# Input stage of a gated attention block: rows turned by diagonal matmuls, a second copy of x already transposed, and two more gate chunks computed there

## The chip, the cores and the metric

One NeuronCore of a Trainium2 chip runs the whole kernel. The metric is the device time of one execution in microseconds, lower is better; it is given as the median of repeated runs.

## The reference

The block takes x of 2048 tokens by 1024 features. All matrices and x are float32. In short:

```python
h = rms_norm(x, norm_gain)                      # per token, then a gain per feature
proj = h @ w_in                                 # 1024 -> 8448 columns
qa, ka, va, qb, kb, vb, ga, gb, mg = split(proj)
ya = banded_attention(qa, ka, va, ...) * silu(ga)      # ga: 512 columns
yb = three_dilated_groups(qb, kb, vb, ...) * silu(gb)  # gb: 512 columns
gates = sigmoid(mg + b_merge)                   # two gates of 1024 columns
merged = gates[0] * (ya @ w_branch_a) + gates[1] * (yb @ w_branch_b)
out = x + merged @ w_out
```

The columns of ga and gb, 1024 in all, are cut into eight **gate chunks** of 128. The change moves chunks 2 and 3 (the second half of ga).

## The kernel before, in words

Every large product is made in float16 with both factors split into a high and a low half: XH and XL hold the normed x, transposed (feature chunks of 128 on the partitions, 2048 tokens along the free axis), and a product takes three matmuls: high by high, high by low, low by high. The program has four stages, one after the other on PE.

**Input stage.** It makes XH and XL and computes gate chunks 0 and 1. x arrives in 16 slabs of 128 tokens (`x_load`), with two gate weights (`g_load`) and the first unit's weights among them. For a slab: ACT squares it with a sum (`x_square`), DVE and ACT make the reciprocal root (`x_stats`, `x_guess`, `x_newton`), DVE multiplies the slab by that and by the gain in one pass of 1024 columns (`x_scale`), PE transposes it in eight blocks through the identity matrix (`x_turn`), ACT copies each half of four blocks to XH (`x_hi`), DVE subtracts to get XL (`x_lo`). Between these PE works on eight gate steps (`g_step`): a chunk of 128 columns over a quarter of 512 tokens, 24 matmuls of 512 columns each. After a step ACT takes the tanh, DVE forms (1 + tanh) times the projection (`gate_steps`), and SP stores the result to DRAM (gtd). The order of all this is set by a small planner, `class Order`: each step has an engine, a cost, the steps it waits for and a rank; the planner lays them out in time and emits the instructions in that order. Each engine then works strictly in the order emitted.

**Main stage.** Units of heads: projection, attention, and, per 128 columns of the attention's output, a turned copy to DRAM (ytd). `YPart` multiplies chunks 0 and 1 by their stored gates there; chunks 2 to 7 go to ytd without their gate.

**Tail.** The table SEQ lists groups (dc, q): dc 0 to 7 are the merge gates, dc 8, 9 and 10 the gate chunks 2 to 7, two chunks of 128 columns to a dc. A group covers 256 columns by 1024 tokens by seven half-size products of 12 matmuls, 84 matmuls of 512 columns. After the products of a group with dc of 8 or more, `silu` loads the matching block of ytd, applies the gate on ACT and DVE, notes its maximum, and stores it. A second planner, `class Plan`, sets the order. K_AT says over which groups the 16 pieces of branch and output weights are prepared.

**Branch stage.** It multiplies by the branch and output weights and ends the program. Its scale y0 needs the maxima of all gated chunks.

Of the kernel before, what the change touches and what calls it, by code (L numbers as in the profile page):

```python
# [21 lines left out]
F32 = mybir.dt.float32  # L22
# [17 lines left out]
VSC = 2.0 ** -16  # L40
SX = 2.0 ** 8
# [43 lines left out]
STD, W_EARLY, G_TH, G_SI, G_CP, K_AT = 5.2, 24.0, 2.0, 4.0, 1.0, (4, 17)  # L85
# [5 lines left out]
X_LD = ("g", 0, 1, 2, 3, "w0", 4, 5, "w1", 6, 7, 8, 9, 10, 11, 12, 13, "u")  # L91
X_RK = (-35, 21, 20, -9)
X_TR = 0.6
X_NR = (-34, -92, 28)
X_XR = (7, -126, 40, 10)
X_GR = (29, 49)
X_TWO = (0, 1, 2, 2)
X_GF = (6.6, 15.2)
X_TH = (45, 46, 85, 86, 125, 126, 165, 166)
X_US = dict(look=0.25, land=4.3, next=1.45, late=.12, sq=1.14, st=.17, ln=.2, nw=.75, sc=1.24, tr=.8, hi=.5, lo=.62, gs=2.1, pw=1.3,  # L100
            gh=1.06, gl=1.26, mm=.217, th=.6, gt=.63, us=.83, uh=.75, ul=.82, ag=1.0, tl=1.3)
X_AG, H_AT = .9, (.1, .35)
XT_BUFS = 14
# [7 lines left out]
def block_kernel(tc, x, w_units, w_gate, w_mrg, w_out, w_bra, w_brk, gain, qkg, sink, bias_a, bias_b, b_merge, out):  # L111
# [166 lines left out]
    gtd = [dr.tile([128, S], F32, name=f"gtd{c}") for c in range(2)]  # L278
# [46 lines left out]

    def g_sum(c):
        gw[c][3] = norm_sum(gw[c][3][:], 1)

    def g_pow(c):
        raw, gh, gl, ps = gw[c]  # L330
        s, inv = norm_pow(ps)
        ih = ucol()
        V.tensor_scalar(ih[:], inv[:], 0.5 / SX, gp2[0][:], OP.mult, OP.mult)
        gw[c] = (gh, gl, ih, raw, s)

    def g_hi(c):
        gh, gl, ih, raw, s = gw[c]
        A.activation(gh[:], raw, AF.Copy, scale=s[:])

    def g_lo(c):  # L340
        gh, gl, ih, raw, s = gw[c]
        V.scalar_tensor_tensor(gl[:], raw, s[:], gh[:], OP.mult, OP.subtract)
        done.add(("g", c))

    def g_step(c, q):

        gh, gl, ih = gw[c][:3]
        ps = pj_p.tile([128, 512], F32, name="pj")
        ts = slice(512 * q, 512 * q + 512)
        out = []  # L350
        for w, xx in ((gh, XH), (gh, XL), (gl, XH)):
            for ch in range(NCH):
                i = len(out)
                out.append(lambda w=w, xx=xx, ch=ch, i=i: T.matmul(  # L354
                    ps[:], lhsT=w[:, ch, :], rhs=xx[:, ch, ts], start=(i == 0), stop=(i == 23)))
        return out, gate_steps(ps, c, q, ih, None)

    def gate_steps(ps, c, q, ih, m):
        th = []

        def tanh():
            th.append(gp.tile([128, 512], F32, name="yo", bufs=3))
            if m is None:
                A.activation(th[0][:], ps[:], AF.Tanh, scale=ih[:])
# [47 lines left out]
    sp0 = st.enter_context(tc.tile_pool(name="sp0", bufs=1))  # L412
    qg = cst.tile([128, 4, HD], F32, name="qg")
# [20 lines left out]

    groups = {t: tuple(i for i in range(4) if X_TWO[i] == X_TWO[t]) for t in range(4)}
    groups.update((t, tuple(range(t - t % 4, t - t % 4 + 4))) for t in range(4, NT))

    def x_square(t):
        g = groups[t]
        if t == g[0]:  # L440
            xss[g] = [sm.tile([128, 4], F32, name="xss")]
        jk = sp0.tile([128, D], F16, name="jk")
        A.activation(jk[:], xts[t][:], AF.Square, accum_out=xss[g][0][:, t - g[0]:t - g[0] + 1])

    def x_stats(g):
        ss = xss[g][0][:, :len(g)]
        V.tensor_scalar(ss, ss, 1.0 / (D * SX * SX), EPS / (SX * SX), OP.mult, OP.add)
        xss[g] = [ss]

    def x_guess(g):  # L450
        if g[0] == 12:
            A.preload_act_table_set("natural_log_exp_and_others")
        xss[g].append(rs_guess(xss[g][0], len(g)))

    def x_newton(g):
        ss, y = xss[g]
        xss[g] = sm.tile([128, 4], F32, name="xr")
        r = xss[g][:, :len(g)]
        rs_newton(ss, y, r, len(g), False)
        V.tensor_scalar(r, r, gi2[0][:], None, OP.mult)  # L460
# [5 lines left out]
    gb = sp0.tile([128, D], F32, name="gb")  # L466

    def gain_load():
        nc.sync.dma_start(out=gb[:], in_=gain.broadcast_to([128, D]))

    def gain_scale():
        m = sm.tile([128, 1], F32, name="gm")
        V.tensor_reduce(m[:], gb[:], AX.X, OP.max, apply_absolute_value=True)
        s, i = pow2(m[:], "x")
        gp2.append(ucol())
        gi2.append(ucol())
        V.tensor_scalar(gp2[0][:], i[:], 2.0 ** 14, None, OP.mult)
# [38 lines left out]
    class Order:  # L516


        def __init__(self):
            self.steps, self.end, self.free, self.on = {}, {}, {}, {}  # L520

        def add(self, name, eng, us, deps, rank, f, *args, first=0.0):
            assert name not in self.steps
            self.on[name] = eng
            self.steps[name] = (eng, us, deps, rank, f, args, first)

        def start(self, name):
            eng, _, deps, _, _, _, first = self.steps[name]
            if any(d not in self.end for d in deps):
                return None  # L530
            late = X_TR if name[0] == "tr" and name[1] > 3 else X_US["late"]
            return max([first, self.free.get(eng, 0.0)] + [self.end[d] + (0 if self.on.get(d) == eng else late) for d in deps])

        def run(self):
            while self.steps:
                best = {}
                for n, s in self.steps.items():
                    t = self.start(n)
                    if t is not None:
                        best.setdefault(s[0], []).append((t, s[3], n))  # L540
                eng, c = min(best.items(), key=lambda e: min(e[1])[0])
                t0 = min(c)[0]
                t, _, n = min((x for x in c if x[0] <= t0 + (0 if eng == "T" else X_US["look"])), key=lambda x: x[1])
                eng, us, _, _, f, args, _ = self.steps.pop(n)
                self.end[n] = self.free[eng] = t + us
                at(t, f, *args)

    od = Order()
    us_ = X_US
    n = 0  # L550
    for k in X_LD:
        for i in range(4 if k == "u" else 1):
            f, args = {"g": (gain_load, ()), "u": (w_load, (0, (i,)))}.get(k, (x_load, (k,)))
            if k in ("w0", "w1"):
                f, args = g_load, (int(k[1]),)
            at(.001 * n, f, *args)
            od.end["ld", k, i] = us_["land"] + us_["next"] * n
# [1596 lines left out]
```

## Time and profile before

| | |
|---|---|
| median of three runs | 1904.86 us (1904.34 to 1906.05) |
| span of the profiled execution, first to last instruction | 1902.2 us |
| time of the profiled execution itself | not listed apart; the median lies 2.7 us above its span |
| PE busy | 1871.2 us, 98% of the span |
| DVE, ACT, POOL busy | 79%, 66%, 31% |
| chain that ended last, by engine | PE 91%, DMA 5%, DVE, ACT and issue 1% each |
| first matmul of the main stage | 80.74 us |

A busy share is the time in which an engine had an instruction in flight. The chain is followed back from the last instruction: at each step to what released it. A timeline row gives its start and duration in us, then engine, line, operation, output and inputs, shape, count, and in brackets the idle time before it and what ended that.

### The profile page before, as it was taken

How to read it: one execution, taken by the hardware profiler on the slowest of the kernel's cores; microseconds unless marked ns; L12 is line 12 of the kernel's file. 1: busy time of each engine (PE TensorE's matmuls, PEld its weight loads, DVE VectorE, ACT ScalarE, POOL GpSimd, SP SyncE). 2: the span in 40 equal slices, each digit the busy share in tenths (PEclk: the TensorE clock that was granted, in tenths of full speed). 3: DMA queues.
4: the chain of work that ended last, by engine and by line, in shares of the span. 5: the costliest groups of instructions: out<-in, count | busy, mean ns of one | idle time of the engine just before them, and what ended most of it. 6: DMA issues, size and time to landing. Idle time of an engine off the chain costs nothing.

```text
span 1902.2 us, 51103 instructions
## 1 busy us (share of the span) xinstructions
PE 1871.2 (98%) x19254; PEld 1439.5 (76%) x19254; DVE 1499.1 (79%) x3837; ACT 1249.0 (66%) x3015; POOL 581.6 (31%) x1363
## 2 busy tenths in 40 slices
PE   6999999999999999999999999999999999999999
PEld 4568987889999899998999899544444446776775
DVE  7679878986886889878789888748779644987885
ACT  8478768886777777777777766565666865433341
POOL 0034343443453435543455444300000000322121
PEclk9999999999999999999999999999999999999999
DMA  6259998987888779888897777776666648854442
GB/s 257 83 103 203 168 194 137 199 168 157 171 148 180 140 155 202 146 166 176 142 176 145 146 153 134 172 300 184 202 201 187 191 154 274 295 162 121 143 149 76
DMA packets 638983, 326.21 MB, mean 171 GB/s; under 512 B 458768, under 2 KB 589712, under 8 KB 636304
## 3 DMA queue, kind: packets, MB, share of 16 engines
q1 hardware_dynamic: 638592, 322.69, 73.1%
q8 instruction: 150, 2.46, 0.6%
q14 instruction: 97, 0.79, 0.1%
q10 hardware_dynamic: 144, 0.26, 0.0%
HBM read 139.08 MB, written 73.66 MB: 112 GB/s over the span
## 4 chain that ended last, share of the span: by engine, by line
PE 91%; DMA 5%; DVE 1%; ACT 1%; issue 1%; SPq 0%; POOL 0%; DVEq 0%; POOLq 0%
PE pj L693 43%; PE fps L1607 18%; PE fps L1927 8%; PE fps L2012 7%; PE s L846 5%; PE pv L895 4%; PE pj L354 2%; DMA pt<-p 2%; PE pj L306 2%; DMA kq<-spl 1%; PE fps L306 1%; PE pt L959 1%; DMA bigl<-sd 1%; DMA graw<-in_w_gate_dram 0%; PE s L484 0%
## 5 line engine op out<-in xcount | busy, mean ns | idle before, releaser
L693 PE MATMUL pj<-wl,XH 128*128 128x128 f16 (+2 forms) x2816 | 715.2, 268 | 0.0
L693 PE MATMUL pj<-wh,XL 128*128 128x128 f16 (+2 forms) x2816 | 711.6, 269 | 0.0
L693 PE MATMUL pj<-wh,XH 128*128 128x128 f16 (+2 forms) x2816 | 708.6, 268 | 0.0
L693 PEld LDWEIGHTS <-XH 128*128 128x128 f16 x5632 | 574.9, 112 | 54.1
L693 PEld LDWEIGHTS <-XL 128*128 128x128 f16 x2816 | 315.8, 112 | 23.8
L861 DVE CUSTOM_DVE_ANT_0 pr<-s,b,ubuf 128x256 f32<-128x256 f32 (+3 forms) x512 | 218.7, 464 | 39.1 <-PE s L846 36.1
L878 DVE SCALAR_TENSOR_TENSOR p<-pr,p 128x512 f16<-128x512 f32 (+2 forms) x256 | 195.9, 765 | 49.7 <-ACT p L874 48.4
L760 POOL TENSOR_TENSOR rw<-rw,g 128x128 f32<-128x128 f32 (+1 forms) x224 | 149.2, 686 | 198.8 <-DVE rw L753 177.8
L1937 POOL TENSOR_TENSOR g<-g,t 128x512 f32<-128x512 f32 x32 | 48.4, 1514 | 522.1 <-DVE t L1859 521.6
L1607 PEld LDWEIGHTS <-wh 128*128 128x128 f16 x1064 | 104.2, 99 | 123.4 <-issue 0.3
L711 ACT ACTIVATE rw<-pj 128x256 f32<-128x256 f32 (+1 forms) x224 | 87.4, 390 | 135.8 <-PE pj L693 135.3
L775 POOL COPY spl<-spl 128x256 f16<-128x256 f16 (+1 forms) x224 | 97.4, 464 | 241.8 <-DVE spl L770 241.8
L874 ACT ACTIVATE p<-pr 128x512 f16<-128x512 f32 (+2 forms) x256 | 157.6, 616 | 10.7 <-DMA pt<-p 6.3
L846 PE MATMUL s<-kq 128*128 128x128 f16 (+1 forms) x1984 | 151.1, 217 | 2.7 <-DMA kq<-spl 1.6
L1927 PE MATMUL fps<-y,bigh 128*128 128x128 f16 x1792 | 153.4, 219 | 0.0
L1927 PE MATMUL fps<-y,bigl 128*128 128x128 f16 x896 | 151.7, 219 | 0.0
L2012 PE MATMUL fps<-WO,mf 128*128 128x512 f16 x660 | 147.5, 379 | 0.0
L846 PEld LDWEIGHTS <-kq 128*128 128x128 f16 x2016 | 131.0, 98 | 18.9 <-issue 3.5
L1927 PEld LDWEIGHTS <-bigh 128*128 128x128 f16 x1792 | 139.0, 98 | 7.3
L895 PE MATMUL pv<-vt,pt 128*128 128x65 f16 (+1 forms) x2784 | 131.6, 193 | 5.7 <-DMA pt<-p 5.7
L895 PEld LDWEIGHTS <-pt 128*128 128x128 f16 x3024 | 119.5, 97 | 21.0 <-DMA pt<-p 8.1
L766 ACT ACTIVATE spl<-rw 128x512 f16<-128x512 f32 (+1 forms) x112 | 72.0, 643 | 79.3 <-POOL vt L722 67.4
(255 smaller groups left out, 3804.6 us busy)
## 6 DMA issues: line engine op xcount, KB each, us to landing
wraw<-in_w_units_dram SPq DMA_DIRECT2D x56, 384.0 KB, 4.5
g<-mgd SPq DMA_DIRECT2D x64, 256.0 KB, 5.1
wraw<-in_w_mrg_dram SPq DMA_DIRECT2D x45, 256.0 KB, 4.3
mgd<-t SPq DMA_DIRECT2D x43, 256.0 KB, 2.8
zd<-z SPq DMA_DIRECT2D x128, 66.0 KB, 2.0
zz<-zd SPq DMA_DIRECT2D x64, 132.0 KB, 3.4
xt<-in_x_dram SPq DMA_DIRECT2D x16, 512.0 KB, 8.0
ytd<-yo SPq DMA_DIRECT2D x32, 256.0 KB, 3.3
```

What stands on the lines that cost most here:

```text
L693: out.append(lambda lhs=lhs, rhs=rhs, ch=ch, a=a, b=b, k=k: T.matmul(ps[:, a:b], lhsT=lhs[:, ch, :], rhs=rhs[:, ch, a:b], start=(k == 0), ...
L711: A.activation(self.rw[:, n * i:n * i + n], self.ps[i][:, :n], AF.Copy)
L760: G.tensor_tensor(q[:, i, :un.nq, :], q[:, i, :un.nq, :], g, OP.mult)
L775: G.tensor_copy(sp[:, i, nh:, :, :], sp[:, i, nq:nh, ::-1, :])
L846: T.matmul(self.sv[j][:, o:o + k1 - k0], lhsT=q[:, h, :], rhs=kt[:, un.nq + kh + v * un.nk, k0:k1], start=(v == 0), stop=(v == 1))
L861: V.tensor_tensor_reduce(out=self.pv[:, j, self.p0:self.p0 + W], in0=self.sv[j], in1=un.bias[:, self.h0 + j, self.b0:self.b0 + W], scale=I ...
L874: A.activation(self.sp[:, :128 * n], self.pr, AF.Copy, scale=PSC)
L878: V.scalar_tensor_tensor(self.sp[:, 128 * n:], self.pr, PSC, self.sp[:, :128 * n], OP.mult, OP.subtract)
L895: T.matmul(self.po[:, j, :w], lhsT=p[:, n * j + s, :], rhs=un.v[key][:, vh, c0:c0 + w], start=(k == 0 and s == 0), stop=(k == 2 and s == n ...
L1607: T.matmul(b[k][:], lhsT=w[:, i, ch, :], rhs=xform(PROD[i][0], lo, ch, q), start=(i < 3 and n == 0), stop=(n == 11), skip_group_check=True)
L1927: out.append(lambda p=p, c=c, wl=wl, yl=yl, n=n: T.matmul(ps[:, 128 * p:128 * p + 128], lhsT=w[wl][:, i, c, p, :], rhs=y[:, yl, c, :], sta ...
L2012: out.append(lambda p=p, ml=ml, wl=wl, k=k: T.matmul(ps[:], lhsT=m[:, ml, p, :], rhs=WO[:, i, wl, p, :], start=(fresh and k == 0), stop=(k ...
```

## The change

- The gain arrives as 128 by 8, one number per partition and feature chunk, and is a scalar of the later passes. The power of two that scales it comes from a root mean square instead of a maximum, and the constants SX and VSC change with it.
- The host also hands in x transposed (xt). The first 512 tokens are still loaded as rows and turned: `x_diag` puts the 128 reciprocal roots of a slab on a diagonal, and `x_turn` multiplies the raw slab by this diagonal, a plain float32 matmul in place of the transpose, so `x_scale` is gone. The blocks of one feature chunk of all four slabs share a bank of 512 columns; `x_hi0` and `x_lo0` take it with the gain as scale.
- The other 1536 tokens are taken from xt, in quarters of 512 tokens (`t_load`, four loads of 512 KB each). Their rows are loaded too, for the sums of squares alone. `x_row` multiplies the diagonal by a matrix of ones, which spreads the reciprocal roots along the free axis of a bank; `x_mul` multiplies a chunk of xt by gain and root; `x_hi` and `x_lo` split two chunks at a time.
- The square of slab 3 moves to DVE; the roots of quarters 2 and 3 come from three Newton steps on DVE instead of Ln and Exp on ACT.
- Gate chunks 0 to 3 are computed in the input stage (NSI = 4): 16 gate steps instead of eight. The four steps of the first quarter may be interleaved; chunks 2 and 3 use the two other banks there.
- dc 10 is gone from SEQ, and dc 8 and 9 now cover chunks 4 to 7: 17 groups instead of 19. Chunks 2 and 3 are gated in the tail by `late`: load ytd and gtd, multiply, maximum, store, eight times, one in each of eight groups. K_AT ends at group 15 instead of 17.
- `Order` now takes the order of ACT and DVE from a table written out by hand (X_SEQ); PE and the queues are still planned.

```diff
+NSI, NY = 4, 2
-SEQ = ((1, 0), (1, 1), (8, 0), (8, 1), (2, 0), (2, 1), (9, 0), (9, 1), (3, 0), (3, 1), (10, 0), (10, 1), (4, 0), (4, 1),
+SEQ = ((1, 0), (1, 1), (8, 0), (8, 1), (2, 0), (2, 1), (9, 0), (9, 1), (3, 0), (3, 1), (4, 0), (4, 1),
...
-X_LD = ("g", 0, 1, 2, 3, "w0", 4, 5, "w1", 6, 7, 8, 9, 10, 11, 12, 13, "u")
+X_LD = ("g", 0, 1, "w0", 2, 3, "w1", "w2", "w3", 4, 5, 6, 7, "t1", 8, 9, 10, 11, "t2", 12, 13, 14, 15, "u", "t3")
+X_SEQ = {
+    "A": (
+        "g0 sq.0 sq.1 ln.0 ln.1 gq.0 sq.2 gq.1 ln.2 gq.2 gh.0 h0.0 gq.3 h0.1 h0.2 h0.3 h0.4 gh.1 h0.5 h0.6 h0.7 gh.2 sq.5 sq.6 sq.7 sq.4 ln.4 gh.3 "
...
+    def t_load(q, i):
+        if i == 0:
+            xtt[q] = sp0.tile([128, NCH, 512], F32, name="xq", bufs=XT_BUFS)
+        nc.sync.dma_start(out=xtt[q][:, i:i + 2, :], in_=xt[i:i + 2, :, 512 * q:512 * q + 512].rearrange("c p t -> p c t"))
-    def x_scale(t):
-        i = t - groups[t][0]
-        V.scalar_tensor_tensor(xts[t][:], xts[t][:], xss[groups[t]][:, i:i + 1], gb[:], OP.mult, OP.mult)
-    def x_turn(t, h):
-        xps[t, h] = ps = s_p.tile([128, 4, 128], F32, name="s")
-        for c in range(4):
-            cc = 4 * h + c
-            T.transpose(ps[:, c, :], xts[t][:, 128 * cc:128 * cc + 128], idf[:])
+    def x_row(t):
...
+        T.matmul(rps[q][:, 128 * i:128 * i + 128], lhsT=ones[:], rhs=dgs[t][:], start=True, stop=True)
+    def x_turn(t, c):
...
+        T.matmul(xch[c][:, 128 * t:128 * t + 128], lhsT=xts[t][:, 128 * c:128 * c + 128], rhs=dgs[t][:], start=True, stop=True)
+    def x_hi0(c):
+        A.activation(XH[:, c, 0:512], xch[c][:], AF.Copy, scale=gs[:, c:c + 1])
+    def x_lo0(c):
+        V.scalar_tensor_tensor(XL[:, c, 0:512], xch[c][:], gs[:, c:c + 1], XH[:, c, 0:512], OP.mult, OP.subtract)
+    def x_mul(q, c):
+        v = xtt[q][:, c, :]
+        V.scalar_tensor_tensor(v, v, gs[:, c:c + 1], rps[q][:], OP.mult, OP.mult)
...
+    def late(n, r):
+        c, q = NY + n % (NSI - NY), n // (NSI - NY)
...
+        pl.add(N("y"), "V", g_us["sum"], [N("ld")], r,
+               lambda: V.scalar_tensor_tensor(t[0][:], t[1][:], gw[c][2], t[0][:], OP.mult, OP.mult))
+        pl.add(N("mx"), "V", g_us["add"], [N("y")], r + 1,
+               lambda: V.tensor_reduce(ymx[:, 4 * c + q:4 * c + q + 1], t[0][:], AX.X, OP.max, apply_absolute_value=True))
...
-    pl.add("y0", "V", 1.0, [n + ("mx",) for n in silus], r, lambda: ym.append(y_scale()))
+    pl.add("y0", "V", 1.0, [n + ("mx",) for n in silus + zs], r, lambda: ym.append(y_scale()))
```

How the order of PE changes at its first gate step. Before, from its first instruction on (s is a bank that receives turned blocks, idf the identity, pt a bank for sums):

```order
L484 MATMUL s<-idf,xt 128x128 x16
L191 MATMUL pt<-gsq,ones 128x1
L484 MATMUL s<-idf,xt 128x128 x8
L191 MATMUL pt<-gsq,ones 128x1
L484 MATMUL s<-idf,xt 128x128 x8
L354 LDWEIGHTS gh
L354 MATMUL pj<-XH,gh 128x512
```

All blocks of the first four slabs are turned, 32 in number, then the first gate step begins. PE now, the last of the turned blocks of the first quarter and the first gate matmul (dg is a diagonal; pj, s and pv are banks of three pools):

```order
L535 MATMUL pj<-dg,xt 128x128 x4
L535 MATMUL s<-dg,xt 128x128 x3
L535 MATMUL pv<-dg,xt 128x128 x2
L535 MATMUL s<-dg,xt 128x128 x3
L535 MATMUL pv<-dg,xt 128x128
L198 MATMUL pt<-gsq,ones 128x3
L535 MATMUL pv<-dg,xt 128x128
L372 LDWEIGHTS gh
L372 MATMUL pj<-XH,gh 128x512
```

The first gate matmul again stands behind the turned blocks: 28 of the 32, since the last feature chunk waits for a bank; those blocks are plain matmuls on dg now. After the first quarter PE has no turned blocks at all, only four matmuls on a diagonal per quarter.

DVE before, at the second quarter's first slabs (rs_t, xr: Newton step; XL: the low half; gl: a gate weight's low half):

```order
L271 TENSOR_TENSOR rs_t<-rs_y 128x4
L272 SCALAR_TENSOR_TENSOR rs_t<-rs_t,xss 128x4
L273 SCALAR_TENSOR_TENSOR xr<-rs_t,rs_y 128x4
L460 TENSOR_SCALAR xr<-xr,ubuf 128x4
L464 SCALAR_TENSOR_TENSOR xt<-xt,xr,gb 128x1024 x2
L342 SCALAR_TENSOR_TENSOR gl<-graw,ubuf,gh 128x1024
L464 SCALAR_TENSOR_TENSOR xt<-xt,xr,gb 128x1024
L491 TENSOR_TENSOR XL<-s,XH 128x4x128 x3
L464 SCALAR_TENSOR_TENSOR xt<-xt,xr,gb 128x1024
```

DVE now, at the same quarter (xq is a piece of the transposed copy, yo a gate):

```order
L496 TENSOR_SCALAR xss<-xss 128x4
L278 TENSOR_TENSOR rs_t<-rs_y 128x4
L279 SCALAR_TENSOR_TENSOR rs_t<-rs_t,xss 128x4
L280 SCALAR_TENSOR_TENSOR xss<-rs_t,rs_y 128x4
L362 SCALAR_TENSOR_TENSOR gl<-graw,gps_286,gh 128x1024
L545 SCALAR_TENSOR_TENSOR xq<-xq,gs,s 128x512 x6
L496 TENSOR_SCALAR xss<-xss 128x4
L545 SCALAR_TENSOR_TENSOR xq<-xq,gs,s 128x512 x2
L389 SCALAR_TENSOR_TENSOR yo<-yo,pj 128x512
```

Four passes of 1024 columns over slabs have become eight of 512 over chunks, and the low halves of a quarter now follow all eight instead of alternating with them.

## Rows read from the trace of the kernel before

**Rows 1.** The page, part 1: busy time by engine.

```profile
PE 1871.2 (98%) x19254; PEld 1439.5 (76%) x19254; DVE 1499.1 (79%) x3837; ACT 1249.0 (66%) x3015; POOL 581.6 (31%) x1363
```

**Rows 2.** Chain of waits in the tail: start, us, what.

```profile
1343.84 36.28 PE fps L1607 x168
1380.23 36.42 PE fps L1607 x168
```

**Rows 3.** Timeline of PE in the input stage.

```profile
10.38 1.94 PE L484 MATMUL s<-idf,xt 128*128 128x128 f32 x8 [10.38 <-DVE xss L447]
...
22.83 3.57 PE L354 MATMUL pj<-XH,gh 128*128 128x512 f16 x8 [0.80 <-ACT XH L487]
26.20 2.06 PE L354 MATMUL pj<-XL,gh 128*128 128x512 f16 x8
...
30.46 1.04 PE L484 MATMUL s<-idf,xt 128*128 128x128 f32 x8
...
40.39 1.89 PE L354 MATMUL pj<-XH,gh 128*128 128x512 f16 x8 [1.73 <-ACT XH L487]
...
79.01 1.89 PE L354 MATMUL pj<-XH,gl 128*128 128x512 f16 x8
80.74 0.33 PE L693 MATMUL pj<-wh,XH 128*128 128x384 f16 x1
```

**Rows 4.** Windows: stretch and length, PE, PEld, DVE, ACT, POOL busy, clock, DMA share, GB/s.

```profile
20.00:30.00 10.00, 9.11 (x33) 4.55 (x34) 8.83 (x20) 9.90 (x19) 0.00 (x0) 1.00 1.03 418
30.00:40.00 10.00, 8.65 (x56) 5.93 (x55) 7.35 (x11) 8.67 (x18) 0.00 (x0) 1.00 0.20 78
```

**Rows 5.** Timelines of DVE and ACT, first loads to the first reciprocal root.

```profile
5.02 1.22 DVE L473 TENSOR_REDUCE gm<-gb 128x1 f32<-128x1024 f32 x1 [5.02 <-DMA gb<-in_gain_dram]
...
8.50 0.16 DVE L273 SCALAR_TENSOR_TENSOR xr<-rs_t,rs_y 128x1 f32<-128x1 f32 x1
...
6.28 1.06 ACT L443 ACTIVATE jk<-xt 128x1024 f16<-128x1024 f32 x1 [4.26 <-DMA xt<-in_x_dram]
7.24 0.19 ACT L443 ACTIVATION_READ_ACCUMULATOR jk<-xt 128x1 f32 x1
```

**Rows 6.** Line 191, input stage: plain float32 matmuls, duration ns min/median/max.

```profile
L191 PEld LDWEIGHTS pt<-gsq,ones x4: 333/333/337, 14.5 to 19.4; 128*128 128x128 f32 x4
L191 PE MATMUL pt<-gsq,ones x4: 208/282/352, 14.7 to 19.4; 128*128 128x1 f32 x4
L191 PEld LDWEIGHTS pt<-wsq,ones x2: 186/188/189, 48.2 to 48.3; 128*128 128x128 f32 x2
```

**Rows 7.** Groups by line, 0 to 82 us: count, busy us, mean ns, idle before.

```profile
L484 PE MATMUL s<-idf,xt 128*128 128x128 f32 x128 | 21.2, 311 | 14.2 <-DVE xss L447 10.4 <-DVE wm L198 2.5 <-DVE xt L464 1.0
L491 DVE TENSOR_TENSOR XL<-s,XH 128x512 f16<-128x512 f32 x32 | 20.6, 683 | 4.4 <-ACT XH L487 4.4
L464 DVE SCALAR_TENSOR_TENSOR xt<-xt,xr,gb 128x1024 f32<-128x1024 f32 x16 | 20.1, 1279 | 0.1
L487 ACT ACTIVATE XH<-s 128x512 f16<-128x512 f32 x32 | 18.2, 595 | 6.3 <-PE s L484 5.9
L443 ACT ACTIVATE jk<-xt 128x1024 f16<-128x1024 f32 x16 | 16.8, 1053 | 4.4 <-DMA xt<-in_x_dram 4.3
L364 ACT ACTIVATE yo<-pj,ubuf 128x512 f32<-128x512 f32 x8 | 5.5, 688 | 11.1 <-PE pj L354 11.0
L371 DVE SCALAR_TENSOR_TENSOR yo<-yo,pj 128x512 f32<-128x512 f32 x8 | 5.5, 681 | 9.7 <-ACT yo L364 9.7
```

**Rows 8.** Windows of the tail, columns as in the windows above.

```profile
1290.00:1330.00 40.00, 40.00 (x189) 18.24 (x187) 33.03 (x64) 22.35 (x41) 0.00 (x0) 1.00 0.56 163
1370.00:1410.00 40.00, 40.00 (x188) 18.35 (x187) 33.62 (x68) 22.97 (x46) 0.00 (x0) 1.00 0.67 192
```

**Rows 9.** Groups by line, 1230 to 1600 us: gating of a stored block.

```profile
L1575 DVE TENSOR_REDUCE ymx<-yr 128x1 f32<-128x512 f32 x24 | 16.2, 679 | 0.2
L1567 DVE TENSOR_TENSOR yr<-t,yr 128x512 f32<-128x512 f32 x12 | 8.2, 684 | 0.1
```

More of the change, by code (lines that the diff above doesn't have):

```diff
@@ L349, in g_step @@
[L349 to L356, printed above, removed]
+        ps = pv_p.tile([128, 512], F32, name="pv") if q == 0 and c > 1 else pj_p.tile([128, 512], F32, name="pj")
@@ L358, in gate_steps, with mm @@
+        def mm(k):
+            w, xx = ((gh, XH), (gl, XH), (gh, XL))[k // NCH]
+            ch = k % NCH
+            T.matmul(ps[:], lhsT=w[:, ch, :], rhs=xx[:, ch, 512 * q:512 * q + 512], start=(k == 0), stop=(k == 23))
+        return mm, gate_steps(ps, c, q, ih, None)
     def gate_steps(ps, c, q, ih, m):
@@ L445, in x_stats @@
[L445 to L460, printed above, removed]
@@ L527, in start @@
         def start(self, name):
-            eng, _, deps, _, _, _, first = self.steps[name]
+            eng, _, deps = self.steps[name][:3]
             if any(d not in self.end for d in deps):
                 return None
-            late = X_TR if name[0] == "tr" and name[1] > 3 else X_US["late"]
-            return max([first, self.free.get(eng, 0.0)] + [self.end[d] + (0 if self.on.get(d) == eng else late) for d in deps])
+            return max([self.free.get(eng, 0.0)] + [self.end[d][0] + (0 if self.end[d][1] == eng else X_US["late"]) for d in deps])
@@ L534, in run @@
         def run(self):
[L535 to L545, printed above, removed]
+            seq = {e: [tuple(int(x) if x.isdigit() else x for x in n.split(".")) for n in X_SEQ[e].split()][::-1] for e in X_SEQ}
@@ new lines, in run @@
+            rest = {e: {n: s[3] for n, s in self.steps.items() if s[0] == e} for e in "TSQ"}
+            while any(seq.values()) or any(rest.values()):
+                best = []
+                for e, l in seq.items():
+                    if l and self.start(l[-1]) is not None:
+                        best.append((self.start(l[-1]), 0, l[-1]))
+                for e, l in rest.items():
+                    c = [(self.start(n), k, n) for n, k in l.items() if self.start(n) is not None]
+                    if c:
+                        best.append(min(c, key=lambda x: x[:2] + (str(x[2]),)))
+                t, _, n = min(best, key=lambda x: x[0])
+                eng, us, _, _, f, args = self.steps[n]
+                self.end[n] = t + us, eng
+                self.free[eng] = t + us
+                if eng in seq:
+                    seq[eng].pop()
+                else:
+                    del rest[eng][n]
@@ L546, in run @@
                 at(t, f, *args)
     od = Order()
+    od.free["Q"] = X_US["land"] - X_US["next"]
     us_ = X_US
@@ L578, in block_kernel @@
-    for c in range(2):
-        r = X_GR[c]
-        od.add(("gq", c), "A", us_["sq"], [("ld", f"w{c}", 0)], r, g_square, c, first=X_GF[c])
-        od.add(("gm", c), "T", .15, [("gq", c)] + ([("gp", 0)] if c else []), r, g_sum, c)
-        od.add(("gp", c), "V", us_["pw"], [("gm", c), "gs"], r, g_pow, c)
-        od.add(("gh", c), "A", us_["gh"], [("gp", c)], r, g_hi, c)
-        od.add(("gl", c), "V", us_["gl"], [("gh", c)], r + 9, g_lo, c)
-    gates = [(q, c) for q in range(4) for c in range(2)]
+        if k == "g":
+            at(.001 * n, gain_load)
+            od.end["ld", "g", 0] = 4.0, "Q"
+            n += 1
+            continue
@@ L586, in block_kernel @@
+    gates = [(q, c) for q in range(4) for c in range(NSI)]
     steps = {}
     def gate_mm(i, k):
+        q, c = gates[i]
         if k == 0:
-            steps[i] = g_step(gates[i][1], gates[i][0])
-        steps[i][0][k]()
+            steps[i] = g_step(c, q)
+        steps[i][0](k)
     def gate_after(i, k):
@@ L1646, in block_kernel @@
         w_steps(dc)
+    lates = iter(range(4 * (NSI - NY)))
     for g in range(LAST):
         group(g)
+        if 0 < g and SEQ[g][0] < 8:
+            n = next(lates, None)
+            if n is not None:
+                late(n, tau(g, 3))
+                z_last = g
     std_steps(7, tau(LAST, 0) - 12, [("d", 7, 3)])
```

328 lines of the change are left out of this document (213 added, 115 removed), and 8 rows, old and new, of the table X_SEQ.

## The prediction

> **What bounds the kernel now.** I read the busy times first: PE has work in flight for 98% of the span [rows 1], so the question is what PE has to do and where it stands still. The chain of waits answers for the tail: two groups there are 168 matmuls in 36.28 us, and the next 168 follow at once [rows 2]. That is 0.216 us for a matmul of 512 columns, and no wait between them: PE's own work sets the tail's length, and work taken out there shortens the program by its full duration as long as no feed becomes late. The timeline of PE in the input stage [rows 3] shows the other kind of stretch. PE starts at 10.38, after a chain of loads, squares and roots; turns 32 blocks; starts its first gate matmul at 22.83; then mixes gate matmuls with turned blocks, with waits of at most 1.73 us, until 80.74, when the main stage begins. Only before 22.83 is there much idle time to fill. The windows show why loads don't bound the stage: they run at 418 GB/s until about 30 us and then all but stop, at 78 GB/s [rows 4].
>
> One more thing must be read off the timeline. The first eight gate matmuls take 3.57 us, 0.45 each; later eight take 1.73 us from start to start (79.01 to 80.74), 0.216 each [rows 3]. The factor two is TensorE's lower level, 1.2 instead of 2.4 GHz, although the clock column says 1.00 [rows 4]. The turned blocks show it too: eight take 1.94 us at 10.38 and 1.04 us at 30.46 [rows 3], 0.24 and 0.13 each.
>
> **The change, part by part. Tail.** Two groups of 84 matmuls go: -36.3 us [rows 2]. Their squares, splits, sums, tanh passes and stores on ACT, DVE and SP go with them. Added are eight late steps. Each is a multiplication and a maximum on DVE, about 0.68 us each by the like passes [rows 9], 1.4 us in a group of 18.1 us, and three transfers of 256 KB, one more than a removed gating had. The 16 weight pieces are pressed from 13 group lengths into 11. In the fullest windows DVE is busy for 33.0 and 33.6 of 40 us [rows 8], and DMA for 0.56 and 0.67, so there is room for both. I cost this at nothing; its cover is the free sixth of DVE. If that is gone, a group's last sum comes late, and PE waits at the next bank. The bound of that is below.
>
> **Input stage, the start.** The gain load is now 4 KB, so slab 0 takes its place. The first 512 KB load landed at 5.02 and the next at 6.28 [rows 5], 1.26 apart, which agrees with 418 GB/s. Slabs 0 and 1 then land at 5.0 and 6.3; behind a gate weight, slab 3 lands fifth, at 10.1, as before. A square is 1.05 and 0.19 on ACT [rows 5, 7]; from the end of slab 0's sum (7.43) to its root (8.66) it took 1.2 [rows 5]. So slab 0's diagonal stands near 8.5, as DVE has the gain's own steps before it. Slab 3, squared on DVE in about 1.3 (a pass of 1024 columns, 1.28 [rows 7]), is done at 11.4; but the guess for slabs 2 and 3 stands on ACT behind the square of the second gate weight, which lands at 11.3 and ends at 12.5. Root 13.7, diagonals 14.1.
>
> In front of the first gate matmul PE has 28 turned blocks, half of them from 8.5 on, half from 14.1 on. Their price is not in the trace. A plain float32 matmul is: the sum at line 191 shows as two records and two weight loads for each call (four of each for two calls), a transpose as one (128 for 16 slabs of eight) [rows 6, 7]. From below it costs what a transpose does at the higher level, 0.13; from above its two weight loads end to end, 2 x 0.333 early, 2 x 0.188 later [rows 6]. I take twice the transpose, 0.48 at the lower level and 0.26 at the higher, as the records are twice as many. At 0.48 throughout, the first gate matmul starts at 8.5 + 28 x 0.48 = 21.9; at 0.26 it is 14.1 + 14 x 0.26 = 17.7. I take 20.5: PE is busy without a break from 8.5, but the level stayed low through all early blocks before. The bounds are 15.9 (0.13) and 27.3 (0.67).
>
> The page Perfetto Trace Analysis of the Trainium skill (Optimizing Tensor Performance, Transposes) speaks against this edit: a logical transpose should be issued as a transpose and not as a standard matmul. By it the edit gives something away: at a transpose's 0.24 a block the gates would start at 14.1 + 14 x 0.24 = 17.5, and the sum below would come to about 1896. No run here shows that, and the rule leaves out that a transpose needs a slab already scaled, a DVE pass of 1.28 each, which the diagonal saves.
>
> **Input stage, from there on.** PE has 16 gate steps of 24: 384 x 0.216 = 82.9 us; 16 more plain float32 matmuls (four blocks of the last chunk, 12 rows) x 0.26 = 4.2; the weight sum, 0.4. For waits and the slow first matmuls I allow 3, as the largest wait before was 1.73 [rows 3]. The end: 20.5 + 82.9 + 4.2 + 0.4 + 3 = 111.0. The same sum for before, 22.8 + 192 x 0.216 + 1.8 for eight at half pace + 96 x 0.13 + 3 = 81.6, is 0.9 over the 80.74 of the row. So the stage ends 111.0 - 80.7 = 30.3 later.
>
> What covers the other engines there? For one quarter DVE has eight multiplications of 512 columns (0.68 by line 491), four low halves of 1024 (1.28), four gates (0.68) and some 11 short steps of 0.16: 5.4 + 5.1 + 2.7 + 1.8 = 15.0. ACT has four squares (5.0), four copies of 1024 (about 1.1 each), four tanh (2.8) and four diagonals (1.2): 13.4, and at most 4 for the unit's weights. PE has 96 x 0.216 + 1 = 21.7 [rows 3, 7]. Both keep ahead once they are ahead. The tight place is the first quarter's end: its gates end near 43, and ACT must by then have made eight high halves, three gate weights, eight squares and the diagonals before the second quarter's first copy, near 42. Loads: the 16 that the first two quarters need land by 5.0 + 15 x 1.26 = 23.9, or a few us later where slabs 6 and 7 wait for the buffers of slabs 0 and 1; that is early enough. The eight further stores (256 KB each) fall where the loads have stopped.
>
> **Sum.** -36.3 + 30.3 = -6.0. Against the profiled span, 1902.2 becomes 1896.2; against the median, which lies 2.7 above that span, 1904.9 becomes **1898.9**. The measurement tells differences over 0.2%, 3.8 us, from none.
>
> **Rivals.**
> 1. *The higher level comes early.* If the plain matmuls run at 0.26 from 14 us on, the gates start at 17.7 and none is slow: end near 107, time near 1895. For it: PE no longer pauses for 2.5 us between slabs as it did [rows 7]. Against: before, the level had not risen after 12 us of turned blocks [rows 3].
> 2. *The gain is eaten by small waits.* ACT is late for the second quarter, or a stored tanh holds its buffer, or DVE in the tail, denser by its pieces, releases banks late: 2 to 5 us together, time 1901 to 1904, no measurable change. For it: ACT works without a pause at 20 to 30 us (9.90 of 10) [rows 4], and its new order is fixed by hand, so one late step holds all behind it. Against: spare time of a quarter's 21.7 on both engines.
> 3. *The turned blocks cost their weight loads,* 0.67 at the lower level and 0.38 later. The gates start at 27.3 and the 16 others take 6.1; with 5 for waits, since the second quarter then also comes late, the end is 27.3 + 82.9 + 6.1 + 0.4 + 5 = 121.7, 41.0 later: +4.7, time 1909.6. It decides for slower from about 0.6 a block. For it: 333 ns a load [rows 6]. Against: the two loads would have to hide behind nothing, while a transpose's loads hide.
>
> **How the numbers follow.** Forecast 0.51, rival 1 0.13, rival 2 0.28, rival 3 0.08. Faster is forecast and rival 1, 0.64; same 0.28; slower 0.08. The range 1894.0 to 1905.5 holds the forecast, rival 2 and most of rival 1, and leaves out rival 3 and the ends.
>
> **What would show it.** The first main-stage matmul near 111 instead of 80.74; the first gate matmul near 20.5; turned blocks of 0.48 that fall to 0.26; chain pieces of PE without breaks in a tail that is 36 us shorter. The prediction is wrong if the stage ends after 116 or PE shows new waits of over 3 us in the tail.

## The result and the profile after

The changed kernel takes 1909.26 us (median of 20 runs, 1903.31 to 1913.45); the kernel before, in the runs beside it, 1903.23 us (20 runs, 1898.34 to 1906.21). The ratio is 1.0031 with a 95% interval of 1.0023 to 1.0038: slower by 0.3%, where 1898.9 was forecast. The profiled execution of the changed kernel took 1908.05 us, its span 1906.0.

The stages, read off the PE timelines as the first matmul of each (us from the span's start):

| kernel | first gate matmul | main stage | tail | branch stage | end |
|---|---|---|---|---|---|
| before | 22.83 | 80.74 | 1235.07 | 1603.65 | 1902.2 |
| changed | 17.71 | 118.14 | 1273.85 | 1607.26 | 1906.0 |

So the input stage became 37.4 longer (forecast 30.3), the main stage 1.4, the tail 35.2 shorter (forecast 36.3), the branch stage 0.2 longer. PE has work in flight for 1870.3 us, 98% of the span, as before [rows 1].

The PE timeline of the changed kernel's input stage answers to [rows 3]:

```profile
9.04 1.22 PE L535 MATMUL pj<-dg,xt 128*128 128x128 f32 x4 [5.66 <-DVE dg L521]
10.05 0.63 PE L535 MATMUL s<-dg,xt 128*128 128x128 f32 x2
...
14.36 1.06 PE L535 MATMUL pj<-dg,xt 128*128 128x128 f32 x8
15.25 0.83 PE L535 MATMUL s<-dg,xt 128*128 128x128 f32 x6
...
17.71 0.83 PE L372 MATMUL pj<-XH,gh 128*128 128x512 f16 x3
18.74 0.38 PE L372 MATMUL pj<-XH,gh 128*128 128x512 f16 x1 [0.20 <-ACT XH L538]
19.62 1.13 PE L535 MATMUL s<-dg,xt 128*128 128x128 f32 x8 [0.51 <-DVE XL L541]
...
40.01 2.08 PE L529 MATMUL s<-dg,ones 128*128 128x128 f32 x8 [8.68 <-ACT dg L523]
41.88 1.49 PE L372 MATMUL pv<-XH,gh 128*128 128x512 f16 x3
43.16 2.17 PE L372 MATMUL pv<-XH,gl 128*128 128x512 f16 x8
45.16 1.89 PE L372 MATMUL pv<-XL,gh 128*128 128x512 f16 x8
...
69.70 0.39 PE L198 MATMUL pt<-wsq,ones 128*128 128x4 f32 x2 [1.69 <-ACT wl L222]
...
118.14 0.33 PE L802 MATMUL pj<-wh,XH 128*128 128x384 f16 x1
```

The reader sees two things. The start went better than forecast: a turned block (two records) takes 0.5 up to about 12.6 and 0.22 from there (four in the 0.89 from 14.36 to 15.25), and the first gate matmul comes at 17.71, at the full pace. Then, in the first quarter's third chunk, PE stands for 8.68 us until 40.0, and works at half pace for a while: eight records of row broadcasts take 1.87, three matmuls 1.28, eight 2.00, then eight 1.73 again. That is about 1.9 us lost over the wait itself. The windows of the same stretch show it in the granted clock (the column before the DMA share):

```profile
25.00:30.00 5.00, 5.00 (x25) 2.23 (x24) 0.81 (x1) 0.00 (x0) 0.00 (x0) 1.00 1.05 397
30.00:35.00 5.00, 1.33 (x7) 0.39 (x4) 0.00 (x0) 0.67 (x1) 0.00 (x0) 0.85 1.04 411
35.00:40.00 5.00, 0.00 (x0) 0.00 (x0) 0.96 (x5) 4.56 (x11) 0.00 (x0) 0.50 1.02 405
40.00:45.00 5.00, 4.99 (x19) 3.11 (x20) 3.86 (x6) 4.72 (x10) 0.00 (x0) 0.63 0.76 261
```

The DMA queues are full until about 40. ACT stands still from 24 to 34, DVE from 26 to 38, PE from 31 to 40. What they wait for stands in the timeline of SP's queue and of ACT:

```profile
7.76 4.20 SPq L450 DMA_DIRECT2D xq<-in_xt_dram  x4
...
16.72 4.43 SPq L450 DMA_DIRECT2D xq<-in_xt_dram  x4
22.12 2.24 SPq L187 DMA_DIRECT2D wraw<-in_w_units_dram  x4
25.12 18.29 SPq L445 DMA_DIRECT2D xt<-in_x_dram  x10
...
34.33 1.06 ACT L492 ACTIVATE jk<-xt 128x1024 f16<-128x1024 f32 x1 [10.23 <-DMA xt<-in_x_dram]
...
39.57 1.26 ACT L523 ACTIVATE dg<-idf,xss 128x128 f32<-128x128 f32 x4
```

The loads of the third quarter's turned x (16.72) and of the first unit's weights (22.12) wait for no buffer; slabs 6 to 15 do: there are six buffers, and slabs 6 to 9 take those of slabs 0 to 3, whose last blocks are turned at 20.7. So these eight loads stand in the queue ahead of slabs 6 and 7, though the table has them far behind. In the planner's model the load that stands earliest in the table goes next as soon as its buffer is free; SP's queue here served what was issued first: slab 6, issued at 25.12, lands at 34.25, behind the last of the eight at 32.97. The second quarter's squares begin with it at 34.3, and that quarter's roots, diagonals and row broadcasts wait for them.

### The profile page after: what moved, and what is told of

Its sections match the earlier page's. It is cut to its first block, busy times and chain, and to the rows that moved or that the text cites. A ratio compares the mean times of both kernels' runs of the same rounds, so it can differ in the third digit from the quotient of the medians.

```text
span 1906.0 us, 51076 instructions
## 1 busy us (share of the span) xinstructions
PE 1870.3 (98%) x19238; PEld 1437.1 (75%) x19238; DVE 1489.0 (78%) x3824; ACT 1241.2 (65%) x2994; POOL 579.4 (30%) x1363
## 4 chain that ended last, share of the span: by engine, by line
PE 91%; DMA 5%; DVE 2%; ACT 1%; issue 1%; POOL 0%; SPq 0%; DVEq 0%; ACTq 0%; POOLq 0%
PE pj L802 42%; PE fps L1736 16%; PE fps L2063 8%; PE fps L2148 7%; PE s L955 5%; PE pv L1004 4%; PE pj L372 3%; DMA kq<-spl 2%; PE pj L313 2%; DMA pt<-p 2%; PE fps L313 1%; DMA xt<-in_x_dram 1%; PE pt L1068 1%; PE pv L372 1%; DMA bigl<-sd 1%
## 5 line engine op out<-in xcount | busy, mean ns | idle before, releaser
L1736 PEld LDWEIGHTS <-wh 128*128 128x128 f16 x952 | 93.2, 98 | 112.1 <-issue 2.0
```

The lines of the kernel that those rows point to most:

```text
L1736: T.matmul(b[k][:], lhsT=w[:, i, ch, :], rhs=xform(PROD[i][0], lo, ch, q), start=(i < 3 and n == 0), stop=(n == 11), skip_group_check=True)
```

## The experiments

**One theory and its rivals.** Theory A: the order of SP's queue makes slabs 6 and 7 late, and engines that work in a fixed order pass that on. Theory B: the loads' sum, 400 GB/s without a break until 40 us, is the limit, in any order.

**e2b_queue**: two groups of loads, the third quarter's turned x and the first unit's weights, wait until slab 7 is issued.

```diff
+            if k in ("t2","u") and i == 0 or k == "u":
+                free = free + [("is", 7, 0)]
             od.add(("is", k, i), "S", .45, free, n, f, *args)
```

> The changed kernel with two groups of loads moved on the SP queue: the second piece of the transposed copy (t2) and the first unit's weights (u) are issued after slabs 6 and 7 instead of before them. PE's order is the same, row for row. Theory A (the 8.7 us wait of PE at the second quarter's rows is slabs 6 and 7 standing in a first-in, first-out queue behind nine loads that nobody needs yet): slab 6 lands near 25 instead of 34.3, the wait of 8.68 us is gone, with it about 2 us of half-pace matmuls behind it; the first main-stage matmul comes at 107 to 109 instead of 118.1, the time falls by 9 to 11 us, and the kernel is faster than the one before by 3 to 5 us. Theory B (the loads' sum is the cause: 17.5 MB before the last piece): the wait only moves to the second or third quarter, the stage still ends after 115, gain at most 3 us. Theory C (the hand-written order of ACT is too slow for the quarter): wait of over 4 us left at the same place.

Measured: 1910.51 us (5 runs), ratio to before 1.0036 (1.0023 to 1.0048); main stage at 121.22. Its timelines of PE, ACT and SP's queue:

```profile
49.45 3.85 PE L372 MATMUL pj<-XH,gh 128*128 128x512 f16 x8 [7.79 <-DVE xh L511]
...
40.25 1.06 ACT L492 ACTIVATE jk<-xt 128x1024 f16<-128x1024 f32 x1 [9.47 <-DMA xt<-in_x_dram]
...
48.36 3.88 ACT L549 ACTIVATE XH<-xq 128x1024 f16<-128x1024 f32 x4
...
22.14 2.22 SPq L450 DMA_DIRECT2D xq<-in_xt_dram  x4
24.40 5.61 SPq L187 DMA_DIRECT2D wraw<-in_w_units_dram  x4
31.09 11.85 SPq L445 DMA_DIRECT2D xt<-in_x_dram  x6
```

The wait of 8.68 is gone, and one of 7.79 stands 10 us further on, so theory C, a wait left at the same place, isn't what happens. PE's first matmul of the second quarter (49.45) needs ACT's first copy at 48.36; the row names a DVE step that ended nearby. Now slabs 10 and 11 are late, behind the turned x and the weights, and in ACT's hand order the third quarter's squares (40.25) stand ahead of the second quarter's copies; DVE's has their statistics ahead of the last two multiplications. Theory A's mechanism is seen, its forecast of the time was not met: a second place of the same kind took the gain, and the main stage starts 3.1 later than in the changed kernel.

**e2_fifo**: every input load waits for the one before it in the table.

```diff
-    n = 0
+    n, last = 0, []
...
+            if last:
+                free = free + last
+            last = [("is", k, i)]
             od.add(("is", k, i), "S", .45, free, n, f, *args)
```

> The changed kernel with all loads of the input stage issued in the order of its table: slabs 6 and 7 also ahead of the first transposed piece t1, and u after all slabs. Theory A: as the run with t2 and u alone moved, within 1.5 us (stage ends at 107 to 110), since t1 is needed only when the rows are made; if slabs 6 and 7 wait for their buffers until about 20.7 the DMA queue stands idle for some us and t1 lands near 30, which may cost up to 1.5. Theory B: stage ends after 115.

Measured: 1903.95 us (11 runs), ratio 1.0004 (0.9994 to 1.0015); main stage at 113.08. Its PE timeline, then its windows:

```profile
44.83 3.85 PE L372 MATMUL pj<-XH,gh 128*128 128x512 f16 x8 [3.38 <-DVE xh L511]
```

```profile
10.00:20.00 10.00, 9.29 (x66) 8.40 (x66) 7.51 (x24) 8.79 (x17) 0.00 (x0) 1.00 0.66 257
20.00:25.00 5.00, 5.00 (x28) 2.58 (x27) 5.00 (x8) 4.97 (x8) 0.00 (x0) 1.00 0.76 236
```

In table order the queue runs dry: 257 and 236 GB/s, where the changed kernel moved 400 and 348, since the second quarter's turned x waits behind slabs 6 and 7, and these for buffers. The second quarter still comes 3.4 us late, behind the third quarter's squares on ACT. 5.1 us of the stage are gone: the main stage starts between what theory A (107 to 110) and theory B (115 or later) had forecast.

**e3_rows_late**: the second quarter's row broadcasts stand behind all of the first quarter's matmuls on PE.

```diff
-... [("l0", c) for c in range(5)] if q == 1 else []
+... [("l0", c) for c in range(5)] + [("mm", 3, 23)] if q == 1 else []
```

> The changed kernel with the four row matmuls of the second quarter placed on PE after all gate steps of the first quarter, instead of after the fifth matmul of the third step. Loads as in the changed kernel. Theory A (late slabs): the wait at the rows is gone, as they are ready at 40.0 when PE gets there, but PE then waits for the second quarter's first high halves, near 47.5: a wait of 5 to 7 us in its place, stage end 113 to 116, gain 2 to 5 us. Rival C' (PE's order alone is the cause, the row matmuls stand too early in a strictly ordered queue): no wait of over 2 us is left, stage end 108 to 109, gain 9 to 10 us.

Measured: 1915.08 us (4 runs), ratio 1.0058 (1.0042 to 1.0073); main stage at 122.30. Its PE timeline:

```profile
40.20 3.59 PE L372 MATMUL pv<-XH,gh 128*128 128x512 f16 x8 [4.38 <-ACT gh L358]
...
54.82 3.59 PE L372 MATMUL pj<-XH,gh 128*128 128x512 f16 x8 [6.12 <-DVE yo L389]
```

The matmuls that could now run ahead of the broadcasts did, and then PE stood twice: for 4.38, as the fourth chunk's weight stands on ACT behind the squares of the same late slabs, and for 6.12 at the second quarter, whose work waits for the broadcasts. The kernel is 5.8 us slower than the changed one, where both expectations had a gain. The place of the broadcasts was not the cause.

**e4_no_late**: the late steps that gate chunks 2 and 3 in the tail are left out.

> The changed kernel without the eight late steps in the tail: chunks 2 and 3 stay without their gate and their maximum is left out of the scale. The tail (first matmul of its first group to first matmul of the branch stage) is 333.5 us in the changed kernel, 35.1 shorter than before instead of 36.3. If the late steps cause the missing 1.2 us: 332.3. If the denser weight pieces on ACT and DVE cause it, or the first loads of the tail: 333 to 334. Time within 2 us of the changed kernel.

Measured: one run of 1911.94 us, no shorter than the changed kernel; its tail takes 339.3 us against 333.4. Its longest waits of PE in the tail (line waited for: us in total, times, longest):

```profile
PE fps L1736 <- DMA bigh<-sd: 2.1, 1, 2.1
PE fps L1736 <- ACT t L1745: 2.0, 1, 2.0
```

In the changed kernel these are 0.8 and 0.4. All waits in this tail sum to 5.1 (2.4 in the changed kernel), and the granted clock falls behind two of them (to 0.69 on average from 1281 to 1286); by the clock's shortfall that costs about 3.4 us, an estimate. Without both, the tail takes 331 us with and without the late steps. The changed kernel's own timeline of SP agrees:

```profile
1290.84 0.32 SPq L1698 DMA_DIRECT2D yr<-ytd  x1
```

This is the first load of a late step. The read-back waits end at 1284.4, ahead of it, and behind it PE waits once in the tail, for 0.42. So the late steps cost at most that.

**e5_ld_order**: e2_fifo, and the second quarter's turned x ahead of slabs 6 and 7.

```diff
-X_LD = ("g", 0, 1, "w0", 2, 3, "w1", "w2", "w3", 4, 5, 6, 7, "t1", 8, ...
+X_LD = ("g", 0, 1, "w0", 2, 3, "w1", "w2", "w3", 4, 5, "t1", 6, 7, 8, ...
```

> Edit: every input load waits for the one before it in the table, as in the run with the queue in table order, and in the table the turned x of the second quarter stands ahead of slabs 6 and 7, so that the queue has loads that wait for nothing until the buffers of slabs 0 and 1 come free. Theory A (the order of the queue, with ACT's hand order behind it, made the input stage late): slabs 6 and 7 land by 27, slabs 8 to 11 by 31, ACT squares without a gap over 2 us, PE shows no wait over 2 us between 18 and 106 us, and its clock stays at the higher level from the first gate matmul; the main stage starts at 17.7 + 82.9 + 16 x .26 + 1 to 3 of small waits = 106 to 108, 10 to 12 us ahead of the changed kernel's 118.1, and the time is 1897 to 1900, a ratio to before of .996 to .998. Theory B (the sum of the loads is the limit, at 400 GB/s without a break until 40 us, so any order is late somewhere): a wait of 3 us or more stays, the main stage starts at 113 or later as in the run in table order, ratio 1.000 or more.

Measured: **1898.88 us** (8 runs, 1894.4 to 1900.91), ratio to before 0.997 (0.9958 to 0.9982). The main stage starts at 106.65. Its timelines of PE, SP's queue and ACT:

```profile
31.19 1.05 PE L529 MATMUL s<-dg,ones 128*128 128x128 f32 x8
...
59.98 0.38 PE L198 MATMUL pt<-wsq,ones 128*128 128x4 f32 x2 [0.68 <-ACT wl L222]
...
106.65 0.33 PE L805 MATMUL pj<-wh,XH 128*128 128x384 f16 x1
...
20.19 5.49 SPq L445 DMA_DIRECT2D xt<-in_x_dram  x6
25.73 2.84 SPq L450 DMA_DIRECT2D xq<-in_xt_dram  x4
28.67 5.48 SPq L445 DMA_DIRECT2D xt<-in_x_dram  x4
...
31.46 1.06 ACT L492 ACTIVATE jk<-xt 128x1024 f16<-128x1024 f32 x1 [0.79 <-DMA xt<-in_x_dram]
```

The same bytes and the same instructions with another order of loads (PE's own order, which the planner lays anew, is the same up to the third quarter's row broadcasts and differs in a few places behind them): no row broadcast waits, the largest wait of PE in the stage after 18 us is 0.68, and the stage ends 11.5 us earlier. Theory B falls, and this version beats both kernels.

**e6_act_order**: e2b_queue, and on ACT and DVE the third quarter's squares and statistics behind the second quarter's splitting.

```diff
-... dg.7 sq.11 sq.8 sq.10 sq.9 th.0 hi.1.0 hi.1.1 hi.1.2 hi.1.3 ...
+... dg.7 th.0 hi.1.0 hi.1.1 hi.1.2 hi.1.3 sq.11 sq.8 sq.10 sq.9 ...
-... mu.1.5 st.8 mu.1.4 mu.1.7 gt.0 nw.8 lo.1.0 gt.1 lo.1.2 lo.1.1 lo.1.3 ...
+... mu.1.5 mu.1.4 mu.1.7 gt.0 lo.1.0 lo.1.2 lo.1.1 lo.1.3 st.8 nw.8 gt.1 ...
```

> Edit: the run in which the third quarter's turned x and the first weights wait for slab 7, with one thing more: in the hand orders of ACT and DVE the squares and statistics of the third quarter (slabs 8 to 11) stand behind the splitting of the second quarter instead of ahead of it. The loads stay in the order in which the wait had moved to 41.7 (7.8 us). Theory A (that wait was ACT, standing at slab 8 with the second quarter's splitting queued behind it): it goes, the second quarter starts at 42 or earlier, the main stage starts at 108 to 112 instead of 121.2, and the time is 1898 to 1902. Theory B (the second quarter's own loads or the sum of the loads were late): the wait at 41.7 stays over 4 us, or the same time is lost at the third quarter, and the main stage starts at 117 or later.

Measured: 1901.24 us (11 runs), ratio 0.9986 (0.9978 to 0.9995); main stage at 111.58. Its timelines of PE and ACT:

```profile
50.95 0.38 PE L372 MATMUL pj<-XH,gh 128*128 128x512 f16 x1 [3.63 <-DVE yo L389]
...
36.31 3.90 ACT L549 ACTIVATE XH<-xq 128x1024 f16<-128x1024 f32 x4 [3.14 <-DVE xq L545]
```

The splitting runs at 36.31 instead of 48.36 with the loads as late as in e2b_queue, and 9.6 us of that kernel's input stage are gone. So in e2b_queue it was the fixed orders of ACT and DVE, not the second quarter's loads, that held PE. A wait of 3.63 is left, where the second gating's tanh stands behind the moved squares on ACT. So a late load holds up whatever is queued behind the instruction that waits for it.

**e7b_transpose**: e5_ld_order, with transposes for the 32 turned blocks, to set the rule on transposes against plain matmuls. The diagonal becomes the identity, so the first 512 rows of x stay unscaled: the scaling pass that a transpose needs is left out.

```diff
-T.matmul(xch[c][...], lhsT=xts[t][...], rhs=dgs[t][:], start=True, stop=True)
+T.transpose(xch[c][...], xts[t][...], dgs[t][:])
...
-V.tensor_scalar(dgs[t][:], idf[:], rs_[q][:, i:i + 1], None, OP.mult)
+V.tensor_scalar(dgs[t][:], idf[:], rs_[q][:, i:i + 1], None, OP.min)
```

> Edit: on the kernel with the loads in the repaired order, the 32 turned blocks of the first quarter become transposes in place of plain float32 matmuls; the diagonals are formed at the same places with the same waits, but as the identity (the minimum of 1 and the scale, which is above 1), so the first 512 rows of x stay unscaled: that scaling is left out, nothing else. Theory C (transposes don't bring TensorE to its higher level, plain matmuls do): blocks take .24 each up to the last, the first gate matmul starts at 17.4 to 17.8, no earlier than the 17.73 of the kernel with plain matmuls, and the first ten or so gate matmuls take .43 each instead of .216, so the main stage starts at 107.5 to 109.5 instead of 106.65 and the time is 1 to 3 us longer. Theory D (in the kernel before it was the pauses of up to 2.48 us between its transposes that kept the level low): the blocks fall from .24 to .13 at about 12.6, the first gate matmul starts at 16.0 to 16.6 at .216 each, the main stage starts at 105 to 106, and the time is about 1 us shorter.

Measured: 1903.2 us (10 runs, 1895.94 to 1906.21), ratio 0.9998 (0.9986 to 1.001). The profiled execution was the fastest; its PE timeline:

```profile
14.01 1.11 PE L535 MATMUL pj<-dg,xt 128*128 128x128 f32 x4 [1.43 <-DVE dg L521]
...
17.33 0.99 PE L372 MATMUL pj<-XH,gh 128*128 128x512 f16 x3
...
106.38 0.33 PE L805 MATMUL pj<-wh,XH 128*128 128x384 f16 x1
```

The blocks take 0.21 to 0.24 up to 16.8 and the first gate matmul comes at 17.33, as theory C has it; but only the first few gate matmuls are slow (three in 0.99), and the main stage starts 0.3 earlier than in e5_ld_order, against both theories. Two more executions of the same kernel were profiled:

> Edit: none against the run with transposes for the first quarter's 32 blocks; one more look, since its executions spread from 1895.9 to 1906.2 with mean clocks of .999 to .996, and the profiled one was the fastest. Theory C (transposes leave TensorE at its lower level, and when it rises after them differs between executions): in an execution of mean clock .997 or less the gate matmuls run at .43 each for several us behind 17.3, and the main stage starts 2 to 6 us behind 106.4. Rival (the spread comes from elsewhere): the main stage starts within 1 us of 106.4, and the lower level stands in the main stage or the tail.

> The same look a second time, with the same expectations: Theory C: at a mean clock of .997 or less the gate matmuls run at .43 each for several us behind 17.3 and the main stage starts 2 to 6 us behind 106.4. Rival: the main stage starts within 1 us of 106.4 and the time is lost in the main stage or the tail.

Measured: 1895.28 us, with a mean clock of 1.000 and the main stage at 107.02; and 1902.5 us, clock 0.995, main stage at 106.03. The first, then the second (timeline, and windows of the main stage and the tail):

```profile
17.43 1.91 PE L372 MATMUL pj<-XH,gh 128*128 128x512 f16 x4
```

```profile
13.81 0.66 PE L535 MATMUL pj<-dg,xt 128*128 128x128 f32 x4 [1.44 <-DVE dg L521]
...
19.80 3.94 PE L372 MATMUL pj<-XH,gh 128*128 128x512 f16 x11
...
1271.92 0.58 PE L1739 MATMUL fps<-bigh,wh 128*128 128x512 f16 x1 [2.51 <-DMA bigh<-sd]
```

```profile
224.00:228.00 4.00, 4.00 (x30) 3.15 (x28) 2.25 (x6) 2.96 (x8) 0.00 (x0) 0.57 0.85 190
752.00:758.00 6.00, 5.37 (x58) 4.75 (x58) 3.51 (x14) 2.83 (x10) 1.03 (x4) 0.72 1.01 189
1270.00:1280.00 10.00, 7.25 (x22) 2.90 (x22) 2.04 (x9) 3.95 (x7) 0.00 (x0) 0.66 1.03 415
```

Theory C falls: in the second profile the transposes did reach the higher level (four in 0.5 us from 13.81), and then eleven gate matmuls ran at a lower pace. The rival holds: the input stage of the longer execution is even 1.0 shorter, and its span's 7.2 us lie in the main stage (1158.0 against 1154.0) and at the tail's start, where PE waits 2.51 for the read-back of a spilled block and then works at half pace until about 1279 (tail 337.5 against 333.4). The main stage's 4 us have the same form. Two waits there, of 2.23 and 1.95, are followed by stretches in which the granted clock falls to 0.57 and 0.72 of full speed on average, where the first profile has 1.00. By the clock's shortfall these cost about 1.7 us each, an estimate from the two windows, and the waits sum to 9.0 instead of 8.3.

Why this version's median is 4.3 above that of e5_ld_order, though its input stage isn't longer, is not shown, but the clock points the same way: nine of its ten executions list a mean granted clock of 0.996 to 0.998, the eight of e5_ld_order 0.998 to 1.000. A thousandth of the span is 1.9 us.

## Why the prediction was wrong

1. **Tail.** Forecast -36.3, measured -35.2. The missing 1.1 stand in the waits of PE, nearly all for read-back blocks at the tail's start: 2.0 us in the changed kernel's rows below, and 0.4 for ACT, against 1.4 in all before (last row). No wait is longer than 0.9 us, so the 16 denser pieces did cost next to nothing, as the term of zero had it.

```profile
PE fps L1736 <- DMA bigl<-sd: 1.2, 2, 0.9
PE fps L1736 <- DMA bigh<-sd: 0.8, 1, 0.8
...
PE fps L1736 <- ACT t L1745: 0.4, 1, 0.4
...
PE fps L1607 <- DMA bigl<-sd: 1.4, 3, 0.6
```

2. **The start.** 20.5 forecast, 17.71 measured. The price of a plain float32 block was right (0.48 and 0.26 taken, 0.5 and 0.22 measured), the level was not: it rose at about 12.6, as rival 1 had it. Rival 3 (0.67 and 0.38 a block) is out; that its time, 1909.6, lies next to the measured one is chance. The Trainium skill (Perfetto Trace Analysis, Optimizing Tensor Performance, Transposes) would have transposes here; by it the forecast's sum came to about 1896. In e7b_transpose they brought the main stage 0.3 us forward, without the scaling pass that they need, and the time did not fall, so no run shows that the diagonal gives anything away.

3. **The step that failed** is the one on the loads: "the 16 that the first two quarters need land by 5.0 + 15 x 1.26 = 23.9, or a few us later where slabs 6 and 7 wait for the buffers of slabs 0 and 1; that is early enough". The count left out what the queue takes in the meantime. Eight loads that wait for nothing went ahead; slab 6 landed at 34.25, and PE stood for 8.68 us. It would have been found by writing the issues down in the order in which each one's buffer is free, rather than in the table's order.

4. **The sum of the stage.** 17.71 for the start + 82.9 for the gate matmuls + 3.5 (16 blocks x 0.22) + 0.4 + 11.1 (waits of 0.20, 0.51, 8.68 and 1.69) + 1.9 at half pace = 117.5, and 0.6 remains to 118.14. Against the forecast's 111.0 that is -2.8 for the start, -0.7 for the blocks, +10.0 for the waits and what they do to the clock (13.0 where 3 were allowed), +0.6. With the order repaired the waits are 1.4 instead of 11.1, nothing is lost at half pace, and the same sum gives 105.9; e5_ld_order shows 106.65. The stage's work was costed rightly, the order of its feed was not. That the time of e5_ld_order, 1898.88, is the one forecast for the change is luck: its input stage ends 4.3 before the forecast's 111.0, near rival 1's 107, while its main stage is 3.3 longer than before (1157.6 against 1154.3) and its tail saves 1.0 less. The forecast put the main stage's change at nothing without a word; PE's waits there sum to 11.6 us instead of 8.0, 2.1 of the rise for transposing DMAs and 1.3 for ACT. Why these come later isn't shown.

5. **Rival 2** named ACT's fixed order as the thing that turns one late step into a stop. That holds (e2b_queue, e6_act_order), but it gave 2 to 5 us for it, and the half pace after a stop was in no term. The main stage's 1.4 lies in its waits for transposing DMAs (6.2 and 3.1 in all, 5.7 and 1.6 before). The medians differ by 6.0, the profiled spans by 3.8. Of the changed kernel's 20 executions the profiled one and four others list a mean granted clock of 0.997, eleven 0.996 and four 0.995; they average 1906.7, 1909.1 and 1911.1 us. So the remaining 2 go with a lower clock; where it falls in executions that were not profiled isn't shown.

## What to carry to other kernels

SP's queue served here what was issued first, so a load that waits for a buffer was overtaken by every load that doesn't, and a planner that lets loads overtake by rank plans on data that isn't there. Write down the order of issue with the buffers' release times, and let the loads that wait for nothing fill the time until a buffer comes free, and no more: with eight too many ahead (the changed kernel) a slab landed 10 us behind the forecast, with none (e2_fifo) the queue ran dry. Then look at what stands behind the first consumer on its engine: there a late load is multiplied, and moving the fixed orders of ACT and DVE (9.6 us here) can be worth as much as moving the load.

## What the runs showed of the hardware

- In the input stages of these traces, loads on SP's queue landed in the order of their issue, whatever the table's order: slab 6 of the changed kernel, issued at 25.12, landed at 34.25, 1.3 behind the last of the eight loads ahead of it.
- Long stops of TensorE were followed by a stretch at its lower level, short ones mostly weren't. After 8.68 us that cost 1.9 more here; after 2.51 us at the tail's start, in the second profile with transposes, matmuls at 0.43 each followed, in the window shown with a granted clock of 0.66. After the first 18 us the traces of these runs have eleven stops of 2.51 to 8.68 us, and the granted clock of the 3 us behind each is 0.50 to 0.70. It is 0.58 behind a stop of 1.95 and 0.65 behind one of 2.23 (second profile), but 1.00 behind one of 2.35 in the kernel before and one of 2.11 in e6_act_order; stops of 0.78 and 0.91 at the changed kernel's tail left it at 1.00. And the second profile's slow stretch from 19.2 follows stops of at most 1.44. So the length of a stop alone doesn't decide it.
- The clock column says 1.00 in stretches in which records stand at half pace: 9 to 12.6 in the changed kernel, 17.4 to 19.3 in the first of the two further profiles of e7b_transpose (four gate matmuls in 1.91). There the starts of the records tell the pace, not the column. Before the change, transposes led up to gate matmuls at half pace [rows 3]; here plain float32 matmuls without a pause led up to the full pace, and the three profiles with transposes show some of each, so the kind of instruction alone doesn't decide it.
- Executions of one kernel differ by up to 10 us (1895.94 to 1906.21 in e7b_transpose). A cost that shows in one profile at the tail's start is partly that execution's own: 333.3 to 339.3 us in ten profiles with 17 groups, all with the same products on PE. In all eleven profiles the main stage is 1145.3 to 1146.3 us plus PE's waits there plus the clock's shortfall (one less the mean granted clock, times the stage's length), so the waits and the clock are nearly all that differs between executions.
